# Down projection of an encoder block as one group of 22 pairs, with gate/up units of two k pairs

## The chip, the cores and the metric

The kernel runs on one core of one Trainium2 chip. The metric is the device time of one launch in microseconds. The core has a matrix engine (TensorE, PE in the profile; its weight loads are PEld), VectorE (DVE), ScalarE (ACT), GpSimd (POOL), and SyncE (SP), which here only issues transfers. Each engine works through its own instructions in order; semaphores order the engines against one another.

## What is computed

One layer of an encoder on x of 512 tokens by 2048 channels, in float32: a normalised input projection, two attention mixers, an output projection added to x, and a gated feed-forward block, then a last normalisation. The change touches the feed-forward block and the last normalisation:

```python
h2 = rmsnorm(x, g_ffn[layer])
gate, up = jnp.split(jnp.einsum('bsd,df->bsf', h2, w_gate_up[layer]), 2, axis=-1)
x = x + jnp.einsum('bsf,fd->bsd', jax.nn.silu(gate) * up, w_down[layer])
...
return rmsnorm(x, g_final)
```

The feed-forward width is 5632, that is 44 tiles of 128 ("f-tiles").

## The kernel before

**Precision.** Every float32 operand is split in two: `hi`, a copy in the matmul's float32r type made by ScalarE, and `lo`, the rest, made by VectorE. `mm3` (lines 194 to 196) issues three matmuls, hi·hi, hi·lo and lo·hi. One matmul has a stationary tile of 128 x 128 (tokens of one tile) and 512 moving weight columns.

**Seven products instead of eight.** Gate/up and most of down use Winograd's form of Strassen's scheme on 2 x 2 blocks: the tokens in two halves (tiles 0, 1 and 2, 3), the contraction in pairs of k tiles, the columns in two blocks of 512. `CHAIN` is the order of the seven products, m1, m7, m6, m2, m5, m4, m3. For each of them the activations have a "form" (a sum or difference of blocks, made by `pair_sums`), split in hi and lo and held in `arena`, two tiles of four pairs each; and each weight pair gives a column of its own: m1, m2 and m3 take a weight block as it is, m7, m6, m5 and m4 a difference or sum made by VectorE in place (`weights`, line 751). Results of several products are added up in the same PSUM banks without starting anew: m1, m6, m5, m3 in bank pair z, m7 and m4 in y, m2 in x. Between them the running value is read out, as every partial chain is one of the wanted terms.

**Units.** A list `units` is worked through in order. One `Cols` unit is one product of one pair: a 256 KB load (`Raw`, tag "craw", 24 buffers), its hi split on ScalarE (line 720) and lo split on VectorE (line 723) into one of eight `twin` buffers, and six matmuls (two token tiles by three). `prepare(n)` issues, ahead of unit n's matmuls, the loads of units up to 20 us ahead and the splits of those up to 8 us ahead, by an assumed 1.37 us per unit. `hooks` attach other work to a unit: evictions, sums, silu, transposes.

**Gate/up** (`gate_up_block`): 11 blocks of four f-tiles, each 7 products by 8 pairs = 56 units. In the units after a block its activations are multiplied, transposed on TensorE (`turn`), summed into the forms (`pair_sums`) and stored in DRAM (`forms_dram`) for the first 40 f-tiles; the last four f-tiles are stored plain (`act_dram`).

**Down.** The first 40 f-tiles are 20 pairs in groups of 8, 8 and 4 (`DOWN_PAIRS`), each group by two column blocks of 1024: six blocks of 7 products. `next_forms` loads the forms (512 KB chunks of four pairs, two buffers `fraw`) and splits them into `arena` (lines 877 and 880) while the block before still runs. The residual x1 lies in DRAM (`x1_dram`). After each product ScalarE reads out its two banks, scaled by the row's factor, into an `ev` slot (line 896), and POOL's queue adds it to x1 in DRAM with an accumulating store (line 897): 82 in all. At the end SP's queue reads x1 back (`load_x1`, line 865), and then the last four f-tiles are done as plain products (`last_down`, `finish`): 4 column chunks by 4 token tiles by 4 f-tiles by 3 = 192 matmuls, the last piece in halves, with the final normalisation beside them: x1 plus the product (line 953), its square sum (954), a product with g_final (961), the factor by a power on POOL, the scaling, and the stores.

Of the kernel before, what the change touches and what calls it, by code (L numbers as in the profile page):

```python
# [44 lines left out]
COLS_AHEAD = 8.0  # L45
COLS_LOAD = 20.0
COLS_US = 1.37
PLAIN_WAIT = 5
SPILL_B = 6
TWINS = 8  # L50
RAWS = {"raw": 6, "craw": 24}
W_TILES = {"wi": 12, "wo": 12, "wl": 32}
DOWN_PAIRS = (8, 8, 4)
F_PLAIN = 40
ORDER = ("m1", "m2", "m4", "m5", "m6", "m7", "m3")
# [7 lines left out]
def encoder_block(ctx, tc, x, g_mix, w_in, g_q_a, g_k_a, g_out_a, g_out_b, w_out, g_ffn,  # L63
# [48 lines left out]
    arena = [sp.tile([P, 7, 4, 2, 256], F32R, tag="arena", bufs=2, name=f"arena{i}") for i in range(2)]  # L112

    def home(n):
        i = n // 7
        return arena[i // 4][:, n % 7, i % 4].rearrange("p a b -> p (a b)")
# [534 lines left out]
    def pair_sums(w):  # L651
        def part(n):
            return w[:, n * 256:(n + 1) * 256]
        a_r, a_l, b_l, b_r, s1, s2, s3, s4 = (part(n) for n in range(8))

        def tt(out, x, y, op=OP.subtract):
            nc.vector.tensor_tensor(out, x, y, op=op)
        tt(s1, a_r, b_r, OP.add)
        tt(s3, a_l, a_r)
        tt(s2, s1, a_l)  # L660
        tt(s4, b_l, s2)

    def form_of(form, i):
        m = ORDER.index(form)
        return arena[i // 4][:, m, i % 4, 0], arena[i // 4][:, m, i % 4, 1]
# [4 lines left out]
    def h_side(i, half, apart=False):  # L670
        if half < 2:
            k = 2 * i + half
            c, j = divmod(k, 4)
            ps = bank("x1t")
            for n, t in enumerate((2, 3, 0, 1) if half == 0 else range(NT)):
                nc.tensor.transpose(ps[:, n * P:(n + 1) * P], x1[c][t][:, j * P:(j + 1) * P], ident)
            if half == 0:
                hpart[0] = sp.tile([P, 4 * 512], F32, tag="pair", bufs=1, name=nm("pair"))
            nc.scalar.activation(hpart[0][:, half * 512:(half + 1) * 512], ps, AF.Copy, scale=gf[:, k:k + 1])
        if half == 1:  # L680
            pair_sums(hpart[0])
        if half >= 2:
            src = hpart[0][:, 256:].rearrange("p (f c) -> p f c", c=256)
            hi, lo = (arena[i // 4][:, :, i % 4, j] for j in range(2))
            if half == 2:
                nc.scalar.activation(hi, src, AF.Copy)
            if half == 3 or not apart:
                nc.vector.tensor_tensor(lo, src, f32(hi), op=OP.subtract)  # L688
# [16 lines left out]
    act_dram = [dp.tile([P, 512], F32, tag=f"act{f}", name=f"act{f}") for f in range(F_PLAIN, NFF)]  # L705
    forms_dram = dp.tile([P, 7, F_PLAIN // 2, 256], F32, tag="forms", name="forms")

    class Cols(Unit):
        ahead = COLS_AHEAD
        load_ahead = COLS_LOAD  # L710
        dur = COLS_US

# [4 lines left out]
        def split_hi(self):  # L717
            self.src = self.box.weights(self.form, self.i)
            self.pair = sp.tile([P, 2, 512], F32R, tag="twin", bufs=TWINS, name=nm("tw"))
            nc.scalar.activation(self.pair[:, 0], self.src, AF.Copy)  # L720

        def split_lo(self):
            nc.vector.tensor_tensor(self.pair[:, 1], self.src, f32(self.pair[:, 0]), op=OP.subtract)  # L723
# [4 lines left out]
    class ColBlock:  # L728
        def __init__(self, w, row, lo, pairs, ready=None):
            self.pairs, self.ready = pairs, ready  # L730
            self.ps, self.at = {}, {}

            def raw(i, j, q):
                at = row + (2 * q + i) * P
                return Raw(lambda t: [(w[0, at:at + P, lo[j]:lo[j] + 512], t)], tag="craw", width=512)
            kinds = {"a": (0, 0), "b": (0, 1), "c": (1, 1), "d": (1, 0), "e": (0, 1), "f": (1, 0), "g": (1, 1)}
            self.raws = [{n: raw(i, j, q) for n, (i, j) in kinds.items()} for q in range(pairs)]
            need = {"m1": "a", "m7": "cb", "m6": "ba", "m2": "d", "m5": "ea", "m4": "fb", "m3": "g"}
            order = [(form, q) for form in CHAIN for q in range(pairs)]
            if ready is not None:  # L740
                rest = order[6:8] + order[8:3 * pairs] + order[3 * pairs + 6:]
                order = order[:6] + order[3 * pairs:3 * pairs + 6] + rest
            for form, q in order:
                self.at[form] = len(units)
                units.append(Cols(self, form, q, [self.raws[q][n] for n in need[form]]))

        def weights(self, form, q):
            t = {n: r.t for n, r in self.raws[q].items()}
# [7 lines left out]

        def bank_of(self, form):
# [5 lines left out]
        def multiply(self, u):  # L763
            dst, i = self.bank_of(u.form), u.i
            if self.ready is not None:
                drain_until(lambda: self.ready[i])
            for t in range(2):
                mm3(dst[t], cols(form_of(u.form, i), t * P), (u.pair[:, 0], u.pair[:, 1]),
                    u.form in ("m1", "m7", "m2") and i == 0, i == self.pairs - 1, True)
# [4 lines left out]
    def gate_up_block(f0):  # L774
        box = ColBlock(w_gate_up, 0, (f0 * P, DFF + f0 * P), KD // 2, hf if f0 == 0 else None)
# [34 lines left out]
        def turn(k):  # L810
            ps = bank("at")
            half = k % 2
            for n, t in enumerate((2, 3, 0, 1) if half == 0 and f0 + k < F_PLAIN else range(NT)):
                src = st[("glo", "uhi")[t // 2]][:, t % 2, k * P:(k + 1) * P]
                nc.tensor.transpose(ps[:, n * P:(n + 1) * P], src, ident)
            if f0 + k >= F_PLAIN:
                a = slot("actT")
                nc.scalar.activation(a, ps, AF.Copy)
                nc.sync.dma_start(act_dram[f0 + k - F_PLAIN], a)
                return  # L820
            if half == 0:
                st["pair"] = sp.tile([P, 4 * 512], F32, tag="pair", bufs=1, name=nm("pair"))
            nc.scalar.activation(st["pair"][:, half * 512:(half + 1) * 512], ps, AF.Copy)

        def store(n):
            nc.sync.dma_start(forms_dram[:, :, n], st["pair"][:, 256:].rearrange("p (f c) -> p f c", c=256))
# [5 lines left out]
        silu("m2", 4, "glo", 0)  # L832
        add("m5", 1, "s7", "uhi")
        add("m4", 1, "s6", "ghi")
        silu("m4", 4, "ghi", 1)
        box.after("m3", 1, low)
        box.after("m3", 3, high)
        for k in range(4):
            late = (6, 8, 18, 20)[k]
            box.after("m3", late, lambda k=k: turn(k))  # L840
            if k % 2 and f0 + k < F_PLAIN:
                box.after("m3", late + 2, lambda: pair_sums(st["pair"]))
                box.after("m3", late + 7, lambda k=k: store((f0 + k) // 2))
        return box

    for f in range(0, NFF, 4):
        box = gate_up_block(f)

    act = {}

    class Act:
        def __init__(self, f):
            self.f, self.t = f, None

        def load(self):
            self.t = slot("actf")
            nc.sync.dma_start(self.t, act_dram[self.f - F_PLAIN])

        def split(self):
            act[self.f] = split(self.t, "act")  # L860

    def load_x1(c, rows):
        for t in rows:
            x1.setdefault((c, t), slot("x1"))
            nc.sync.dma_start(x1[c, t], x1_dram[c, t])

    def next_forms(box, first, pairs):
        def ready(form, h):
            m, st = ORDER.index(form), {}
            hi, lo = (arena[h][:, m, :, j] for j in range(2))  # L870

            def load():
                st["t"] = sp.tile([P, 4, 256], F32, tag="fraw", bufs=2, name=nm("fr"))
                nc.sync.dma_start(st["t"], forms_dram[:, m, first + 4 * h:first + 4 * h + 4])

            def split_hi():
                nc.scalar.activation(hi, st["t"], AF.Copy)

            def split_lo():
                nc.vector.tensor_tensor(lo, st["t"], f32(hi), op=OP.subtract)  # L880
            box.after(form, 3 * h - 5, load)
            box.after(form, 3 * h + 1, split_hi)
            box.after(form, 3 * h + 3, split_lo)
        for form in CHAIN:
            for h in range(pairs // 4):
                ready(form, h)

    def down_block(first, pairs, cb, last):
        box = ColBlock(w_down, 2 * first * P, (cb * 1024, cb * 1024 + 512), pairs)

        def add(form, late, i, j):
            def go():
                for t in range(2):
                    row = 2 * i + t
                    e = slot("ev")
                    nc.scalar.activation(e, box.bank_of(form)[t], AF.Copy, scale=r2["r"][:, row:row + 1])  # L896
                    nc.gpsimd.dma_start(x1_dram[2 * cb + j, row], e, accum_op=OP.add)  # L897
            box.after(form, late, go)

        def close():  # L900
            for t in range(2):
                dst = x1[2 * cb + 1, t]
                nc.vector.scalar_tensor_tensor(dst, box.bank_of("m3")[t], r2["r"][:, t:t + 1], dst,
                                               op0=OP.mult, op1=OP.add)
        add("m1", 0, 0, 0)
        add("m7", 0, 1, 1)
        add("m6", 0, 1, 0)
        add("m2", 0, 0, 0)
        add("m5", 0, 1, 1)
        add("m4", 0, 1, 0)  # L910
        if last:
            box.after("m4", -1, lambda: load_x1(3, (0, 1)))
# [208 lines left out]
```

## Time and profile before

| what | before |
|---|---|
| runs | 2056.56, 2057.41, 2057.89 us; median 2057.41 |
| span of the profiled execution (the only time that the profile gives for it) | 2057.2 us |
| matmuls and transposes on TensorE | 9159 |
| last matmul starts | 2048.61 us |
| moved by DMA | 386.39 MB, mean 188 GB/s |

How to read it: a matmul's shown duration overlaps with that of the next, so the pace is read from the starts. The profile's times count from the first instruction. In a row of groups the columns are line, engine, operation, tiles and shapes with the count, then busy us and the mean ns of one, then the idle time of that engine ahead of the group with what ended it. In a row of waits they are the waiting instruction, what released it, and total, number and longest of these waits in us. PEclk is the clock granted to TensorE, 1.00 being full.

### The profile page before, as it was taken

What the parts mean: (1) busy time and instruction counts of PE and PEld (TensorE: products, weight loads), DVE (VectorE), ACT (ScalarE), POOL (GpSimd) and SP (SyncE); (2) the same over time, 40 slices, a digit from 0 to 9 for tenths busy, and PEclk for the clock granted to TensorE, in tenths of its full rate; (3) what the DMA queues carried; (4) which work ended last, traced back from release to release, by engine and by line L of the source; (5) the groups of instructions that cost most, each with busy time, mean ns of one, the idle gap of its engine ahead of it and who ended that gap; (6) DMA issues with size and microseconds to landing.
All of it is one profiled execution on the core that took longest, in us unless ns stands there. A gap on an engine that the chain in (4) does not pass through costs nothing.

```text
span 2057.2 us, 27020 instructions
## 1 busy us (share of the span) xinstructions
PE 2022.3 (98%) x9159; PEld 1660.1 (81%) x9159; DVE 1462.2 (71%) x2566; ACT 1047.1 (51%) x1854; POOL 129.1 (6%) x135
## 2 busy tenths in 40 slices
PE   9999999999999999999999999999999999999897
PEld 7888888888888878888888888888887888788675
DVE  5555755645654698877877878878879878877565
ACT  5334344444534565554555554554556666566453
POOL 3100100000000000000000000000000111111220
PEclk9999999999999999999999999999999999999999
DMA  7322222222433654845835836836748989989974
GB/s 231 109 76 83 87 74 76 73 82 92 153 119 134 214 164 162 309 135 192 316 122 207 299 124 222 288 121 236 274 138 311 276 247 331 315 236 314 241 178 151
DMA packets 227978, 386.39 MB, mean 188 GB/s; under 512 B 20944, under 2 KB 64000, under 8 KB 227840
## 3 DMA queue, kind: packets, MB, share of 16 engines
q1 hardware_dynamic: 213840, 359.43, 51.3%
q0 software_dynamic: 11808, 21.50, 6.5%
q10 hardware_dynamic: 2192, 3.74, 0.5%
q8 instruction: 71, 1.16, 0.2%
q14 instruction: 67, 0.55, 0.1%
HBM read 331.64 MB, written 52.95 MB: 187 GB/s over the span
## 4 chain that ended last, share of the span: by engine, by line
PE 85%; issue 7%; DMA 4%; DVE 2%; POOL 2%; ACT 1%; SPq 0%; POOLq 0%; ACTq 0%; DVEq 0%
PE zc L196 9%; PE zc L194 9%; PE zc L195 9%; PE pj L194 6%; PE pj L195 6%; PE pj L196 6%; PE yc L195 5%; PE yc L196 5%; PE yc L194 5%; PE pw L194 3%; PE pw L196 3%; PE pw L195 3%; PE xc L196 2%; PE xc L195 2%; PE xc L194 2%
## 5 line engine op out<-in xcount | busy, mean ns | idle before, releaser
L720 ACT ACTIVATE tw<-raw 128x512 fp32r<-128x512 f32 x896 | 541.2, 629 | 410.0 <-DVE raw L751 285.2
L723 DVE TENSOR_TENSOR tw<-raw,tw 128x512 fp32r<-128x512 f32 x896 | 599.4, 687 | 206.2 <-ACT tw L720 198.5
L194 PE MATMUL zc<-tw,arena 128*128 128x512 f32 x1024 | 404.5, 395 | 6.2 <-ACT ev L896 6.1
L195 PE MATMUL zc<-tw,arena 128*128 128x512 f32 x1024 | 400.8, 391 | 0.2
L196 PE MATMUL zc<-tw,arena 128*128 128x512 f32 x1024 | 400.9, 392 | 0.0
L751 DVE TENSOR_TENSOR raw<-raw,raw 128x512 f32<-128x512 f32 x512 | 350.8, 685 | 0.0
L194 PEld LDWEIGHTS zc<-tw,arena 128*128 128x128 f32 x1024 | 193.4, 189 | 47.8 <-ACT ev L896 8.6
L194 PE MATMUL pj<-w,arena 128*128 128x512 f32 x576 | 229.3, 398 | 1.2 <-ACT w L232 1.2
L195 PEld LDWEIGHTS zc<-tw,arena 128*128 128x128 f32 x1024 | 193.5, 189 | 41.4 <-DVE tw L723 2.3
L196 PEld LDWEIGHTS zc<-tw,arena 128*128 128x128 f32 x1024 | 193.2, 189 | 41.1 <-DVE arena L688 0.4
L195 PE MATMUL pj<-w,arena 128*128 128x512 f32 x576 | 225.4, 391 | 0.9 <-DVE w L237 0.9
L196 PE MATMUL pj<-w,arena 128*128 128x512 f32 x576 | 225.7, 392 | 0.0
L194 PE MATMUL yc<-tw,arena 128*128 128x512 f32 x512 | 201.2, 393 | 4.4 <-ACT tw L720 4.4
L195 PE MATMUL yc<-tw,arena 128*128 128x512 f32 x512 | 200.9, 392 | 2.4 <-DVE tw L723 2.4
L196 PE MATMUL yc<-tw,arena 128*128 128x512 f32 x512 | 200.0, 391 | 0.0
L237 DVE TENSOR_TENSOR w<-raw,w 128x512 fp32r<-128x512 f32 x192 | 140.8, 747 | 27.0 <-ACT w L232 19.2
L232 ACT ACTIVATE w<-raw 128x512 fp32r<-128x512 f32 x192 | 116.1, 627 | 67.5 <-PE pj L196 29.4
L897 POOL DMA_DIRECT2D x1d<-ev x82 | 72.4, 951 | 1177.8 <-ACT ev L896 1169.4
L194 PEld LDWEIGHTS pj<-w,arena 128*128 128x128 f32 x576 | 108.6, 189 | 23.8 <-ACT w L232 1.4
L196 PEld LDWEIGHTS pj<-w,arena 128*128 128x128 f32 x576 | 108.5, 188 | 23.8 <-DVE arena L189 0.2
L195 PEld LDWEIGHTS pj<-w,arena 128*128 128x128 f32 x576 | 108.7, 189 | 23.4 <-DVE w L237 1.2
L194 PEld LDWEIGHTS yc<-tw,arena 128*128 128x128 f32 x512 | 96.5, 189 | 25.5 <-ACT tw L720 5.7
(189 smaller groups left out, 2633.7 us busy)
## 6 DMA issues: line engine op xcount, KB each, us to landing
raw<-in_w_gate_up_dram SPq DMA_DIRECT2D x616, 256.0 KB, 5.4
raw<-in_w_down_dram SPq DMA_DIRECT2D x280, 256.0 KB, 6.9
x1d<-ev POOLq DMA_DIRECT2D x82, 256.0 KB, 6.8
raw<-in_w_in_dram SPq DMA_DIRECT2D x38, 512.0 KB, 3.8
forms<-pair SPq DMA_DIRECT2D x20, 896.0 KB, 5.3
fr<-forms SPq DMA_DIRECT2D x35, 512.0 KB, 6.0
raw<-in_w_in_dram SPq DMA_DIRECT2D x68, 256.0 KB, 3.0
raw<-in_w_out_dram SPq DMA_DIRECT2D x32, 512.0 KB, 4.2
```

The source lines that it names most:

```text
L194: nc.tensor.matmul(dst, ah, bh, start=start, stop=False, skip_group_check=chained)
L195: nc.tensor.matmul(dst, ah, bl, start=False, stop=False, skip_group_check=chained)
L196: nc.tensor.matmul(dst, al, bh, start=False, stop=stop, skip_group_check=chained)
L232: nc.scalar.activation(self.w[0], src, AF.Copy)
L237: nc.vector.tensor_tensor(self.w[1], self.src, f32(self.w[0]), op=OP.subtract)
L720: nc.scalar.activation(self.pair[:, 0], self.src, AF.Copy)
L723: nc.vector.tensor_tensor(self.pair[:, 1], self.src, f32(self.pair[:, 0]), op=OP.subtract)
L751: nc.vector.tensor_tensor(t[d], t[a], t[b], op=op)
L897: nc.gpsimd.dma_start(x1_dram[2 * cb + j, row], e, accum_op=OP.add)
```

## The change

What it does:

- **Down**: all 44 f-tiles are 22 pairs in one group (`Down`). A unit covers one product of one pair for both column blocks: weights `[P, 2, 512]`, loaded as 512 KB, and 12 matmuls. Products run in braids of two, m1 with m7, m6 with m4, m5 with m2, the second eight pairs behind the first, then m3 alone. The eight banks are z (m1, m6, m5, m3) and y (m7, m4, then m2).
- The block a of each weight pair stays in SBUF from m1 to m5 (`home`, 22 tiles); m7 turns it in place into the column that m6 takes (`between`). All other down loads share the 12 places of three `stock` tiles.
- Forms are loaded in chunks of four pairs just ahead of their use into four `forms_at` tiles.
- m1, m7, m6 and m4 are read out with four accumulating stores each, 16 in all, through two `evs` tiles. m5 and m2 are added from PSUM to x1 tiles, which POOL's queue loads, with g_final, near the end of m5.
- The last four pairs of m3 are held back and done by token tile in `finish`, the last piece in halves in banks of y.
- **Gate/up**: units of two k pairs (`Wides`): 512 KB loads into stock tiles a, b and s of four places each, splits of 128 x 1024, 12 matmuls, four twins. Hooks count in the new units; the arena is divided by form (four and three forms) instead of by pair.

```diff
-DOWN_PAIRS = (8, 8, 4)
-F_PLAIN = 40
-ORDER = ("m1", "m2", "m4", "m5", "m6", "m7", "m3")
+COLS_AHEAD = 8.2
+WIDE_US = 2.72
+PAIRS = NFF // 2
+LAG = 8
+TAIL = 4
+CHUNK = 4
+ORDER = ("m1", "m4", "m5", "m3", "m2", "m7", "m6")
...
+    stock = {k: wp.tile([P, 4, 2, 512], F32, tag="stock" + k, bufs=1, name="stock" + k) for k in "abs"}
+    twins = [sp.tile([P, 2, 2, 512], F32R, tag=f"twin{k}", bufs=1, name=f"twin{k}") for k in range(4)]
...
+        def load(self):
+            if self.tag == "home":
+                self.t = wp.tile([P, 2, 512], F32, tag="home", bufs=PAIRS, name=nm("home"))
+            else:
+                n = turns[self.tag]
+                turns[self.tag] += 1
+                self.t = stock["abs"[n // 4 % 3] if self.tag == "d" else self.tag][:, n % 4]
+            nc.sync.dma_start(self.t, self.src)
...
         def split_hi(self):
             self.src = self.box.weights(self.form, self.i)
-            self.pair = sp.tile([P, 2, 512], F32R, tag="twin", bufs=TWINS, name=nm("tw"))
-            nc.scalar.activation(self.pair[:, 0], self.src, AF.Copy)
+            n = turns["twin"]
+            turns["twin"] += 1
+            self.pair = twins[n % 4]
+            nc.scalar.activation(self.pair[:, :, 0], self.src, AF.Copy)
 
         def split_lo(self):
-            nc.vector.tensor_tensor(self.pair[:, 1], self.src, f32(self.pair[:, 0]), op=OP.subtract)
+            self.box.between(self.form, self.i)
+            nc.vector.tensor_tensor(self.pair[:, :, 1], self.src, f32(self.pair[:, :, 0]), op=OP.subtract)
...
+            for lead, lag in (("m1", "m7"), ("m6", "m4"), ("m5", "m2")):
+                for q in range(PAIRS + LAG):
+                    if q < PAIRS:
+                        order.append((lead, q))
+                    if q >= LAG:
+                        order.append((lag, q - LAG))
+            order += [("m3", q) for q in range(PAIRS)]
...
+            return {"m1": lambda: a, "m7": lambda: tt(t["b"], t["c"], t["b"]), "m6": lambda: a,
+                    "m4": lambda: tt(t["d"], t["d"], a), "m5": lambda: tt(t["c"], t["c"], a),
+                    "m2": lambda: t["d"], "m3": lambda: t["c"]}[form]()
+
+        def between(self, form, q):
+            if form == "m7":
+                a = self.home[q].t
+                nc.vector.tensor_tensor(a, self.raws[form, q]["b"].t, a, op=OP.add)
...
+            hook(first - 7, load)
+            hook(first - 3, hi)
+            hook(first - 2, lo)
...
+            for cb in range(2):
+                e = evs[turns["ev"] % 2][:, cb]
+                nc.scalar.activation(e, box.bank_of(form)[t][cb], AF.Copy, scale=r2["r"][:, row:row + 1])
+                nc.gpsimd.dma_start(x1_dram[2 * cb + j, row], e, accum_op=OP.add)
...
+    for n in range(4):
+        box.after("m5", PAIRS - 4, n, lambda n=n: take_x1(4 * n, 4 * n + 4))
+    box.after("m5", PAIRS - 2, 1, load_gfin)
...
+        add_in(z[1][1], 3, 1)
+        for cb in range(2):
+            run(z[0][cb], 0, cb, 0, 512, False)
+            add_in(z[0][cb], 2 * cb + 1, 0)
+            square(2 * cb + 1, 0)
+        rows_done(0)
+        run(z[1][0], 1, 0, 0, 512, False)
+        for c in (1, 3):
+            give(c, 0)
+        scale_out(0, rf[0])
+        add_in(z[1][0], 1, 1)
+        square(1, 1)
...
+        for n, (lo, hi) in enumerate(((0, 256), (256, 512))):
+            run(y[0][n], 1, 1, lo, hi, True)
+            add_in(y[0][n][:, lo:hi], 3, 1, lo, hi)
...
+            if n == 0:
+                nc.vector.tensor_tensor(early_y1, xd[1, 1], gf_of(1), op=OP.mult)
+                nc.vector.tensor_reduce(pre[:, :1], ssf[:, 4:8], axis=AX.X, op=OP.add)
+                nc.vector.tensor_scalar(pre[:, 1:], pre[:, :1], 1.0 / D, EPS, op0=OP.mult, op1=OP.add)
```

418 lines of the change are left out of this document (229 added, 189 removed).

## The prediction, made before the changed kernel was run

> **What bounds the kernel now.** I read the page first: engine totals, then the largest groups.
>
> ```profile
> span 2057.2 us, 27020 instructions
> PE 2022.3 (98%) x9159; PEld 1660.1 (81%) x9159; DVE 1462.2 (71%) x2566; ACT 1047.1 (51%) x1854; POOL 129.1 (6%) x135
> ```
>
> TensorE (PE) has hardly an idle moment, so only two things can shorten the span: fewer matmuls, or matmuls that start closer together. How close they can be is in the timeline of TensorE in an undisturbed gate/up block (start, duration):
>
> ```profile
> 1005.67 0.39 PE L194 MATMUL zc<-tw,arena 128*128 128x512 f32 x1
> ...
> 1016.55 0.39 PE L194 MATMUL yc<-tw,arena 128*128 128x512 f32 x1
> ```
>
> Between these starts lies one product of a block: eight units of six matmuls, 48 in 10.88 us, **0.2267 us each**. The 0.39 us is the overlapped duration, which is why a busy share of 98% can hide losses. So I cut the stretch from the last gate/up block's m2 to the last matmul into windows (window, length, PE busy (count), PEld, DVE, ACT, POOL, PEclk, DMA share, GB/s) and set each length against its matmuls at 0.2267 us:
>
> ```profile
> 1541.44:1588.81 47.37, 45.52 (x193) 35.57 (x192) 46.27 (x71) 31.97 (x51) 0.00 (x0) 1.00 0.86 301
> 1588.81:1753.96 165.15, 165.15 (x738) 136.71 (x736) 132.42 (x202) 99.42 (x162) 24.96 (x28) 1.00 0.96 287
> 1753.96:1767.24 13.28, 11.75 (x49) 8.85 (x48) 11.11 (x18) 7.62 (x13) 1.76 (x2) 1.00 1.02 342
> 1767.24:1908.68 141.44, 141.44 (x625) 117.16 (x624) 108.96 (x171) 83.53 (x137) 23.84 (x27) 1.00 0.98 282
> 1908.68:1923.70 15.02, 12.20 (x50) 8.59 (x48) 7.50 (x12) 7.14 (x12) 2.62 (x4) 1.00 1.08 329
> 1923.70:1956.86 33.16, 27.59 (x97) 20.84 (x97) 19.81 (x32) 17.58 (x30) 8.71 (x10) 0.85 0.89 188
> 1956.86:1979.08 22.22, 22.19 (x98) 17.87 (x96) 12.23 (x20) 10.38 (x18) 5.26 (x6) 1.00 1.00 273
> 1979.08:1996.12 17.04, 13.06 (x49) 10.07 (x48) 8.18 (x14) 11.07 (x21) 3.48 (x4) 0.90 0.59 81
> 1996.12:2048.61 52.49, 46.21 (x205) 37.61 (x203) 35.33 (x62) 22.16 (x52) 3.42 (x5) 0.93 0.48 150
> 2048.61:2057.20 8.59, 0.28 (x3) 0.07 (x1) 2.13 (x6) 1.84 (x4) 0.55 (x1) 0.81 0.35 122
> ```
>
> Losses, row by row: 192 matmuls need 43.5, 3.8 lost; the second row none (720 matmuls, 163.2, and 16 transposes); 48 need 10.9, 2.4 lost; 624 need 141.5, none; 48: 4.1; 96 (21.8): 11.4; 96: 0.4; 48: 6.1; the last row has 180 whole matmuls and 24 half ones, 43.5, about 8.9 lost. Together **37.1 us**, all in the last gate/up block and the down stage, and in part a lower granted clock (PEclk 0.85 to 0.93) where TensorE had paused. The waits name the causes. First the window of the last two down blocks and the end (waiter <- releaser: total, times, longest), then the window of the last gate/up block:
>
> ```profile
> DVE tw L723 <- ACT tw L720: 44.0, 14, 5.1
> ACT ev L896 <- DMA x1d<-ev: 27.3, 17, 4.1
> PE fd L194 <- ACT w L232: 6.1, 1, 6.1
> PE zc L194 <- ACT ev L896: 6.1, 3, 3.8
> ```
>
> ```profile
> L880 DVE TENSOR_TENSOR arena<-fr,arena 128x1024 fp32r<-128x1024 f32 x9 | 11.0, 1218 | 0.0
> PE yc L195 <- DVE tw L723: 1.3, 3, 0.7
> ```
>
> In the short last blocks (four pairs, 38 us) ScalarE stands 27.3 us before evictions whose buffer an accumulating store still holds; the weight splits queue behind them, VectorE waits for the splits and TensorE for both. Then the read-back of x1 delays the weights of the last four f-tiles (6.1). In the last gate/up block nine splits of down forms add 11.0 us to a VectorE that is busy 46.27 of 47.37.
>
> **The change, part by part.** *Last four f-tiles as two more pairs.* 192 matmuls of the plain product and 1680 of 20 pairs become 22 x 7 x 12 = 1848: 24 fewer, 24 x 0.2267 = **-5.4**. The extra instructions from a halved last piece are 12 before and after: 0.
>
> *Gate/up units of two k pairs.* Same matmuls and bytes, so 0 from this part on TensorE, which has no gaps there. VectorE gains cover. Its timeline shows what an operation really occupies:
>
> ```profile
> 1550.86 0.68 DVE L751 TENSOR_TENSOR raw<-raw,raw 128x512 f32<-128x512 f32 x1
> 1551.46 0.68 DVE L723 TENSOR_TENSOR tw<-raw,tw 128x512 fp32r<-128x512 f32 x1
> 1552.06 1.22 DVE L880 TENSOR_TENSOR arena<-fr,arena 128x1024 fp32r<-128x1024 f32 x1
> 1553.20 0.68 DVE L751 TENSOR_TENSOR raw<-raw,raw 128x512 f32<-128x512 f32 x1
> ```
>
> Start to start a narrow operation takes 0.60 and a wide one **1.14**, less than their durations. A wide unit with a difference costs 2.28 of the 2.72 us that its 12 matmuls take (84%; two narrow ones 2.40). Four twins and three units ahead are as much time as before. The loads c to g of a block share four slots ("s"). The tightest is e: it waits until d of the same index is split, and its difference must start four units later; from 2.4 us into one unit (when that second split ends, below) to 1.2 us before the start of the fourth unit after it are 4 x 2.72 - 3.6 = 7.3 us.
>
> ```profile
> raw<-in_w_gate_up_dram SPq DMA_DIRECT2D x616, 256.0 KB, 5.4
> raw<-in_w_in_dram SPq DMA_DIRECT2D x38, 512.0 KB, 3.8
> raw<-in_w_out_dram SPq DMA_DIRECT2D x32, 512.0 KB, 4.2
> ```
>
> Loads of 512 KB land in 3.8 to 4.2 us, so it holds, with VectorE's lead as a second cover. If that cover were gone it would cost the lateness once per block.
>
> *Form splits leave the last gate/up block* but for one: **-3.8**, and VectorE there falls below TensorE's need.
>
> *Accumulating stores 82 to 16, two buffers of their own.* After each of m1, m7, m6, m4 four evictions, two per unit, at least eight units (21.8 us) before the bank or the buffer is needed again. Stores land in 6.8 us (first row below). The waits for ev, and the pauses behind them, go; so does the read-back in front of weights: x1 and g_final, 5.2 MB, move from SP's queue, where weights stood behind them, to POOL's, where only the accumulating stores, long done, are ahead; 17 issues of 0.95 us run from four units before m5's last one, while weights and forms there ask 241 GB/s (one load of 512 KB and a quarter of a chunk per unit) of the 390 shown below. **-33.3**, the rest of the 37.1.
>
> ```profile
> x1d<-ev POOLq DMA_DIRECT2D x82, 256.0 KB, 6.8
> L897 POOL DMA_DIRECT2D x1d<-ev x82 | 72.4, 951 | 1177.8 <-ACT ev L896 1169.4 <-DMA raw<-in_w_down_dram 7.2 <-DMA fr<-forms 1.2
> ```
>
> *What is late next: VectorE in the first braid.* m1 costs a split (1.14); m7 a difference, the in-place sum for m6, and a split (3.42); a form chunk 1.14 each four units. A pair of units is 4.56 + 0.57 = 5.13 of 5.44 us: it fits. But the braid ends with eight m7 units alone: 8 x 3.42 = 27.4, with chunk splits (1.14, 1.14, 0.6) 30.2, against 21.8 of TensorE: 8.4 short. A twin is free only when its matmuls are done, so a unit's second split ends about a unit start + 2.4 us, three units early: at most 8.16 - 2.4 = 5.8 us of lead. Shortfall 2.6; the last chunk falls into slack behind, and I take **+2.0**. Bounds: 0, if chunks fall outside; 8.4 with no lead.
>
> A rule of the Trainium skill would make this dearer. The page "VectorE: DVE Perf Modes", section "The DRAIN you can't avoid", says the next operation does not start until the pipe has emptied. By it each step takes its full duration, 1.22 us; this gives the rival of full steps below. The rows above show a start 0.08 us before the former's end, so I keep 1.14.
>
> *DMA in that braid.* Three loads of 512 KB per two units and half a chunk are 1.84 MB in 5.44 us, 337 GB/s; the last eight units ask 434 for 21.8 us, with twelve slots filled ahead. What the engines give with the same 2 KB pieces, in one window:
>
> ```profile
> 1000.00:1010.88 10.88, 10.88 (x49) 9.01 (x48) 10.35 (x18) 4.99 (x9) 0.00 (x0) 1.00 1.06 390
> ```
>
> 390 suffices with the slots. The Trainium skill's "DMA: Bandwidth & Descriptors", section "Where 436 GB/s comes from", has HBM bind at about 358 per core; by that figure the braid still fits and the tail lacks 1.6 MB, less than the slots hold. The window is above it.
>
> *The end.* Four m3 units are held back for the finish. At pair 18 the last unit's first split must wait for pair 17's matmuls: 1.05 (first row below) + 1.14 and hand-overs, about 2.6 us, while only nine matmuls (2.0) are left: +0.5. In the finish the scaling of rows t=0 (two operations each on ScalarE and VectorE) stands before t=1's sums, and the partial mean before the last addition: by the durations below the latter is ready some 0.9 us after the last matmul. **+1.4** together, between 0 and 3. The chain after that is the same operations as now: 0.
>
> ```profile
> L877 ACT ACTIVATE arena<-fr 128x1024 fp32r<-128x1024 f32 x35 | 36.9, 1053 | 8.0 <-DMA fr<-forms 8.0
> L953 DVE SCALAR_TENSOR_TENSOR x<-fd,r,x 128x512 f32<-128x512 f32 x15 | 11.2, 748 | 5.8 <-PE fd L196 5.8
> L961 DVE TENSOR_TENSOR y<-x,gfin 128x512 f32<-128x512 f32 x15 | 10.4, 693 | 3.4 <-DMA gfin<-in_g_final_dram 2.1 <-ACT jf L954 0.8
> ```
>
> *Handing memory over.* Stock tiles are bigger single tiles, home tiles lie where the arena's halves were, and a pair's split becomes two pieces per engine. The wait at the change to gate/up is now
>
> ```profile
> PE x1t L676 <- DVE x L621: 0.7, 2, 0.4
> ```
>
> and I add as much again, **+0.7**, from 0 to 4: a load that waits for memory is issued seven units ahead, and the split of a pair in two pieces is hidden behind the out projection for all but the last pair.
>
> Sum: 2057.2 - 5.4 - 3.8 - 33.3 + 2.0 + 1.4 + 0.7 = 2018.8. The median of the runs, 2057.41, is 0.2 above this execution: **2019.0**.
>
> **The rivals.** *Full steps* (5%): at 1.22 us a pair of units takes 5.49 of VectorE against 5.44, which costs 0.7 of lead over 14 pairs, and the eight units with their chunk splits 32.4 against 21.8: 10.6 short, less 5.1 of lead, +5.5 in place of +2.0, **2022.5**. Against: the spacing shown.
>
> *VectorE or the read-back decides* (17%): no lead remains at the m7 tail (+6.4), or x1 and g_final, 5.2 MB beside the weights, cost again the 6.1 that they cost now: 2025. For: VectorE at 5.13 of 5.44 us has no reserve; against: four units between a load's issue and its use.
>
> *DMA bounds the first braid* (13%). Windows of down with accumulation beside it move 282 to 342 GB/s. At 300 each pair of units takes 6.1 instead of 5.44, 9.5 over 14 pairs, and the eight alone 31.5 instead of 21.8, 9.7; the slots' 6.3 MB give some back: up to +19, say +14, with a lowered clock near 2034. Against: 390 without accumulation, of which the first braid has none until its end.
>
> *Slower than before* (4%): the four shared slots. If a 512 KB load landed later than about 7.3 us plus VectorE's 4.6 of free lead, each of the 11 gate/up blocks would stop at its m5. To lose all 38.4 that is 3.5 us per block: it decides from a landing of 11.9 us and turns the sign at 15.4. No median among the rows above is over 6.8. A further 2% is the stalls returning in full elsewhere: within 0.2%.
>
> **How the numbers follow.** Forecast 59% (2014 to 2023), full steps 5%, 2025: 17%, 2034: 13%, same 2%, slower 4%. The range takes forecast and the first rival, and the near part of the second: from 2013.5 (all losses gone and no new one is 2015.1; 1.6 less if wide units shorten the start of gate/up) to 2031. Faster by over 0.2%, about 4 us and what this kernel's runs can tell from none, 94%.
>
> **What would show it.** Right: 0.2267 us between matmuls from 30 us to the end but for some 2 us at the last m7 units, where TensorE waits for VectorE's second split; 24 fewer matmuls; PEclk 1.00 until the last matmul; no waits for ev buffers. Wrong: ScalarE or VectorE waiting for a weight load in the first braid (DMA), pauses in each gate/up block's m5 (slots), or a pause at the x1 loads.

## The result and the profile after

| | before | changed |
|---|---|---|
| four runs of each, median (lowest to highest) | 2057.30 us (2056.56 to 2057.89) | 2023.15 us (2022.11 to 2024.27) |
| span of the profiled execution | 2057.2 us | 2022.5 us |
| last matmul starts | 2048.61 us | 2013.31 us |

The ratio of the times is 0.9834 (95% interval 0.9820 to 0.9848): 1.7% faster. The forecast was 2019.0 us in a range of 2013.5 to 2031. The page of the changed kernel begins:

```profile
span 2022.5 us, 24151 instructions
...
PE 2005.3 (99%) x9135; PEld 1653.4 (82%) x9135; DVE 1429.0 (71%) x1876; ACT 952.6 (47%) x1345; POOL 81.7 (4%) x86
```

TensorE has 9135 instructions for 9159: the 24 matmuls are gone. The windows of the changed kernel, with the columns of the windows before (window, length, PE, PEld, DVE, ACT, POOL, PEclk, DMA share, GB/s), cover the start of gate/up, one whole gate/up block, its last block's m2 to m3, and down to the end:

```profile
742.89:762.36 19.47, 15.90 (x60) 12.30 (x58) 16.29 (x19) 10.16 (x15) 1.86 (x1) 0.82 0.38 140
...
1468.23:1546.35 78.12, 78.12 (x354) 64.63 (x352) 60.20 (x62) 37.26 (x43) 0.00 (x0) 1.00 0.64 212
1546.35:1589.87 43.52, 43.52 (x194) 36.04 (x192) 33.13 (x32) 20.88 (x23) 0.00 (x0) 1.00 0.94 328
1589.87:1686.94 97.07, 97.07 (x437) 80.49 (x436) 90.08 (x86) 48.18 (x50) 0.49 (x1) 1.00 0.92 329
1686.94:1713.63 26.69, 25.64 (x109) 20.03 (x108) 26.69 (x25) 14.16 (x17) 3.78 (x5) 1.00 0.74 218
1713.63:1952.99 239.36, 239.36 (x1057) 198.20 (x1056) 185.50 (x163) 125.39 (x139) 19.14 (x29) 1.00 0.76 253
1952.99:2010.56 57.57, 57.42 (x254) 47.22 (x253) 41.23 (x49) 28.38 (x36) 2.66 (x3) 1.00 0.45 151
2010.56:2013.31 2.75, 2.75 (x25) 2.75 (x23) 2.67 (x5) 1.90 (x4) 0.05 (x1) 1.00 0.39 145
2013.31:2022.50 9.19, 0.28 (x3) 0.07 (x1) 2.46 (x7) 2.41 (x8) 0.54 (x1) 0.64 0.54 185
```

Read each length against its matmuls at 0.2267 us. The last gate/up block's 192 matmuls take 43.52 us, just what they need; they took 47.37 before. In 239.36 us of down there are 1056, which need 239.4: nothing lost, and the clock stays at 1.00. Only four places are not at pace: nine m7 units at the end of the first braid (108 matmuls, 24.5 needed, 26.7 taken: 2.2), the last product (0.4), the end behind the last matmul (9.19 for 8.59), and, not in down at all, the start of gate/up, where 19.47 us hold 60 records and the granted clock is 0.82 in the mean. TensorE's own waits name two of them:

```profile
PE zc L196 <- ACT arena L700: 3.5, 1, 3.5
...
PE yd L197 <- DVE twin L754: 0.9, 3, 0.4
```

So the 37.1 us of old losses are gone, and a new pause of 3.8 us between starts has come at 743 us: TensorE waits there for ScalarE's split of a form.

### The profile page after: what moved, and what is told of

Read it like the earlier page. It is cut to its first block, busy times and chain, and to the rows that moved or that the text cites. A ratio compares the mean times of both kernels' runs of the same rounds, so it can differ in the third digit from the quotient of the medians.

```text
span 2022.5 us, 24151 instructions
## 1 busy us (share of the span) xinstructions
PE 2005.3 (99%) x9135; PEld 1653.4 (82%) x9135; DVE 1429.0 (71%) x1876; ACT 952.6 (47%) x1345; POOL 81.7 (4%) x86
## 4 chain that ended last, share of the span: by engine, by line
PE 95%; DVE 3%; issue 1%; ACT 1%; DMA 0%; ACTq 0%; POOLq 0%; POOL 0%; DVEq 0%
PE zc L198 8%; PE zc L196 8%; PE zc L197 8%; PE pj L196 7%; PE pj L198 7%; PE pj L197 7%; PE yc L196 4%; PE yc L198 4%; PE yc L197 4%; PE zd L197 4%; PE zd L198 4%; PE zd L196 4%; PE pw L196 3%; PE pw L198 3%; PE pw L197 3%; PE yd L198 3%
## 5 line engine op out<-in xcount | busy, mean ns | idle before, releaser
L196 PE MATMUL zc<-twin,arena 128*128 128x512 f32 x704 | 277.8, 395 | 3.5 <-ACT arena L700 3.5
L198 PE MATMUL zc<-twin,arena 128*128 128x512 f32 x704 | 275.3, 391 | 0.0
L197 PE MATMUL zc<-twin,arena 128*128 128x512 f32 x704 | 274.6, 390 | 0.0
L750 ACT ACTIVATE twin<-stockb 128x1024 fp32r<-128x1024 f32 x168 | 178.3, 1062 | 191.1 <-PE zc L198 76.9
L754 DVE TENSOR_TENSOR twin<-stockb,twin 128x1024 fp32r<-128x1024 f32 x168 | 205.1, 1221 | 40.8 <-ACT twin L750 38.8
L754 DVE TENSOR_TENSOR twin<-stocks,twin 128x1024 fp32r<-128x1024 f32 x126 | 154.2, 1224 | 103.6 <-ACT twin L750 103.2
L750 ACT ACTIVATE twin<-stocka 128x1024 fp32r<-128x1024 f32 x124 | 131.5, 1061 | 170.9 <-PE xc L198 58.3
L754 DVE TENSOR_TENSOR twin<-stocka,twin 128x1024 fp32r<-128x1024 f32 x124 | 151.5, 1223 | 66.5 <-ACT twin L750 58.5
L750 ACT ACTIVATE twin<-stocks 128x1024 fp32r<-128x1024 f32 x126 | 133.4, 1059 | 133.1 <-PE yc L198 71.4
L196 PEld LDWEIGHTS zc<-twin,arena 128*128 128x128 f32 x704 | 132.4, 188 | 30.7 <-ACT arena L700 3.8
L198 PEld LDWEIGHTS zc<-twin,arena 128*128 128x128 f32 x704 | 132.4, 188 | 28.9 <-DVE arena L702 0.8
L197 PEld LDWEIGHTS zc<-twin,arena 128*128 128x128 f32 x704 | 132.6, 188 | 26.3
L196 PE MATMUL yc<-twin,arena 128*128 128x512 f32 x352 | 138.6, 394 | 0.0
L198 PE MATMUL yc<-twin,arena 128*128 128x512 f32 x352 | 137.6, 391 | 0.0
L197 PE MATMUL yc<-twin,arena 128*128 128x512 f32 x352 | 137.5, 391 | 0.0
L197 PE MATMUL zd<-twin,form 128*128 128x512 f32 x348 | 135.5, 389 | 0.1
L196 PE MATMUL zd<-twin,form 128*128 128x512 f32 x348 | 135.6, 390 | 0.0
L198 PE MATMUL zd<-twin,form 128*128 128x512 f32 x348 | 135.4, 389 | 0.0
```

Of the source, the lines that this page charges most:

```text
L196: nc.tensor.matmul(dst, ah, bh, start=start, stop=False, skip_group_check=chained)
L197: nc.tensor.matmul(dst, ah, bl, start=False, stop=False, skip_group_check=chained)
L198: nc.tensor.matmul(dst, al, bh, start=False, stop=stop, skip_group_check=chained)
L750: nc.scalar.activation(self.pair[:, :, 0], self.src, AF.Copy)
L754: nc.vector.tensor_tensor(self.pair[:, :, 1], self.src, f32(self.pair[:, :, 0]), op=OP.subtract)
```

## The experiments

Unless it says otherwise a time is the span of one profiled execution, to be set against 2022.5 (changed) or 2057.2 us (before). Spans of one kernel differ by some us: the four of the changed kernel lie between 2020.3 and 2022.5, ten more of the kernel before between 2052.3 and 2056.4, so both figures are at the long end of their kind. In the runs below the part ahead of gate/up, which no edit touches, alone ends anywhere from 722.7 to 724.7 us. So where a span says one thing and the window of the edited stage another, the window decides.

### Where the new pause comes from

The last three times that TensorE makes a half-pair of the feed-forward input (four transposes in a row), from its timeline of the kernel before, then of the changed one:

```profile
728.88 0.60 PE L676 MATMUL x1t<-ident,x 128*128 128x128 f32 x4
734.80 0.60 PE L676 MATMUL x1t<-ident,x 128*128 128x128 f32 x4
736.62 0.60 PE L676 MATMUL x1t<-ident,x 128*128 128x128 f32 x4
```

```profile
729.69 0.60 PE L688 MATMUL x1t<-ident,x 128*128 128x128 f32 x4
741.06 0.60 PE L688 MATMUL x1t<-ident,x 128*128 128x128 f32 x4
742.89 0.60 PE L688 MATMUL x1t<-ident,x 128*128 128x128 f32 x4
```

These transposes are tasks of the `side` queue, which gives out one task after each unit. A unit has twice the matmuls now, so the queue runs at half its pace: from the first of the rows to the second, with other tasks between them, pass 5.9 us before and 11.4 after.

```diff
-        if side:
-            side.popleft()()
+        for _ in range(2 if isinstance(u, Wides) else 1):
+            if side:
+                side.popleft()()
```

> The changed kernel, with two tasks of the side queue per wide unit instead of one. Theory: the 3.8 us pause at 743 us and the slow restart come from the side queue, which gives out one task per unit while a unit is now twice as long, so that the last pair of the feed-forward input is transposed at 742.9 us instead of 736.6. Then the last transposes move to about 737 us, the pause goes, and the span falls from 2022.5 to about 2017.5 us. Rival: the pause comes from the new division of the arena or the split in two pieces; then the pause of 3 us or more stays and the span stays within 1 us of 2022.5.

Measured 2016.9 us, 5.6 less. The last transposes start at 736.39 us in its timeline. From the first matmul of gate/up to the end of the first m7 it takes 32.9 us, 5.7 less than the changed kernel. One wait of 1.05 us is left there, 12 matmuls (2.72 us) in 3.77:

```profile
742.30:746.07 3.77, 3.23 (x14) 2.10 (x12) 3.73 (x7) 3.09 (x5) 0.00 (x0) 1.00 1.05 404
```

The theory holds; the new division of the arena and the split in two pieces, which stay in this run, are not the cause of the 3.8 us.

### The end of the first braid

VectorE is busy for the whole of the window 1686.94 to 1713.63 above, 26.69 of 26.69 us. Its timeline there shows the spacing of the wide operations:

```profile
1697.56 1.21 DVE L917 TENSOR_TENSOR stocka<-stocka 128x1024 f32<-128x1024 f32 x1
1698.69 1.22 DVE L926 TENSOR_TENSOR home<-stocka,home 128x1024 f32<-128x1024 f32 x1
1699.83 1.21 DVE L754 TENSOR_TENSOR twin<-stocka,twin 128x1024 fp32r<-128x1024 f32 x1
1700.96 1.21 DVE L917 TENSOR_TENSOR stockb<-stockb 128x1024 f32<-128x1024 f32 x1
```

Difference, sum for m6, split, and the next unit's difference: starts 1.13 to 1.14 us apart, 3.40 us a unit where TensorE needs 2.72. Two runs test that VectorE, and not the loads, sets the pace. The first shortens the stretch in which m7 stands alone:

```diff
-LAG = 8
+LAG = 4
```

> The changed kernel with the second product of a braid four pairs behind the first instead of eight. Theory (VectorE is short in the m7 units that stand alone): with four alone the shortfall is 4 x 0.7 plus chunk splits, under the lead of 5.8 us, so the waits of TensorE for VectorE there (2.2 us) go: span about 2020.3. Rival (the first braid's weights come late): four units alone still ask for 434 GB/s, but for 10.9 us only; the waits would fall too, but ScalarE or VectorE would be seen waiting for a load.

Measured 2018.5 us. The window of its five m7 units at the end:

```profile
1695.66:1709.26 13.60, 13.60 (x62) 11.26 (x61) 13.56 (x13) 9.20 (x12) 3.79 (x5) 1.00 0.91 195
```

60 matmuls in 13.60 us is full pace, with VectorE busy 13.56 of them: the lead just suffices. The 2.2 us are gone: down takes 421.3 us from its first matmul to its last, where the changed kernel takes 423.4. The rest of the difference is not the edit's: 2.2 us less ahead of down, 0.4 more behind the last matmul. The second run adds to VectorE's work and to nothing else:

```diff
-                nc.vector.tensor_tensor(self.pair[:, :, 1], ...)
+            for _ in range(2 if self.form == "m7" and isinstance(self.box, Down) else 1):
+                nc.vector.tensor_tensor(self.pair[:, :, 1], ...)
```

> The changed kernel with the low split of each m7 unit of down done twice (same result). Theory (VectorE bounds the first braid, 1.14 us a step): a pair of braided units takes 6.27 of VectorE against 5.44, 11.6 over 14 pairs, and the eight alone with chunk splits 39.4 against 21.8; less 5.8 of lead that is 23.4 of waiting in place of 2.2, span about 2044. With steps of 1.22 us it would be near 2052. Rival (the weights' loads bound it): VectorE has room, span within 5 us of 2022.5.

Measured 2047.5 us, 25.0 more. The nine units, 24.5 us of matmuls, now take 42.4, with VectorE full and the DMA engines at half load:

```profile
1696.26:1738.64 42.38, 29.42 (x110) 20.73 (x108) 42.07 (x38) 16.27 (x19) 4.61 (x5) 0.96 0.54 155
```

That is VectorE's bound: 22 more operations at 1.14 us are 25.1 us, and 25.0 came (25.6 in down itself). My sum said 21. It let the lead cover all but 5.8 us of what the braid ahead of these nine units loses; there 107.0 us passed where the changed kernel takes 97.1, a loss of 10.0.

A third run took the sum off VectorE:

```diff
-                nc.vector.tensor_tensor(a, self.raws[form, q]["b"].t, a, op=OP.add)
+                nc.gpsimd.tensor_tensor(a, self.raws[form, q]["b"].t, a, op=OP.add)
```

> The changed kernel with the in-place sum that m7 leaves for m6 on GpSimd instead of VectorE. Theory: VectorE has then two steps per m7 unit, 2.28 of 2.72 us, and the 2.2 us at the end of the first braid go: span about 2020.3. If GpSimd's wide sum (a narrow one takes 1.29 us, so 2.6 or more) slows VectorE or comes late for m6: slower than 2022.5.

Measured 2048.2 us: a miss, 25.7 more instead of 2.2 less. VectorE's and GpSimd's timelines of that run:

```profile
1719.32 1.21 DVE L754 TENSOR_TENSOR twin<-stocka,twin 128x1024 fp32r<-128x1024 f32 x1
1720.45 3.39 DVE L917 TENSOR_TENSOR stockb<-stockb 128x1024 f32<-128x1024 f32 x1
1723.77 1.21 DVE L754 TENSOR_TENSOR twin<-stocka,twin 128x1024 fp32r<-128x1024 f32 x1
```

```profile
1719.53 3.23 POOL L926 TENSOR_TENSOR home<-stocka,home 128x1024 f32<-128x1024 f32 x1 [2.36 <-issue]
1723.93 3.32 POOL L926 TENSOR_TENSOR home<-stockb,home 128x1024 f32<-128x1024 f32 x1 [1.17 <-DVE stockb L917]
```

GpSimd's sum runs from 1719.53 to 1722.76. VectorE's difference starts in that time and takes 3.39 us in place of 1.21: it ends 1.1 us after the sum, as if it had begun only then. The relief was paid back with the time of the other engine's instruction. In the same run a split of 8.13 us stands beside three sums in a row; it ends 1.1 us after the last of them, which takes 2.44 us, the least of all 22 sums:

```profile
1710.13 8.13 DVE L754 TENSOR_TENSOR twin<-stocks,twin 128x1024 fp32r<-128x1024 f32 x1
1714.73 2.44 POOL L926 TENSOR_TENSOR home<-stocka,home 128x1024 f32<-128x1024 f32 x1
```

### What the old losses in down were

First four runs of the kernel before with one edit each, then one with two of these edits together and one of the changed kernel.

```diff
-                    e = slot("ev")
+                    e = sp.tile([P, 512], F32, tag="ev", bufs=8, name=nm("ev"))
```

> The kernel before, with eight buffers of their own for evictions instead of places among the shared slots. Theory (evictions wait for a buffer that an accumulating store holds, and the splits queue behind them): the 27.3 us of ScalarE's waits for buffers fall to a few, and of the 24 us lost in the last two down blocks most comes back: span 2057.2 to about 2037. Rival (the DMA engines are overloaded by accumulation and form loads, buffers are only where it shows): the wait moves to weight loads, span above 2050.

Measured 2033.0 us: 24.2 less from eight buffers of 2 KB per partition. The evictions' waits for a buffer held by a store are gone, and the blocks of four pairs, which had lost 22 us, run at pace, with all 82 accumulating stores still there and the DMA engines as busy as before: 312 of their 336 matmuls in 70.72 us (first row).

```profile
1906.24:1976.96 70.72, 70.72 (x314) 58.56 (x312) 53.40 (x87) 50.38 (x87) 22.63 (x26) 1.00 1.04 276
1731.52:1758.32 26.80, 23.55 (x98) 19.02 (x96) 14.85 (x23) 13.67 (x22) 3.54 (x4) 0.94 1.00 317
1976.96:2024.53 47.57, 45.56 (x205) 37.47 (x203) 32.18 (x56) 19.31 (x46) 1.66 (x3) 0.96 0.55 189
```

What is left, besides the last gate/up block, is a loss of 5.0 us from 1743 us on, between the second and the third block, where the first product waits for its banks to be read out (second row, 96 matmuls), and 4.0 us at the last four f-tiles (third row, 43.5 needed), of which TensorE's wait for the last weights is 2.0.

```diff
-                    nc.gpsimd.dma_start(x1_dram[2 * cb + j, row], e, accum_op=OP.add)
+                    nc.gpsimd.dma_start(x1_dram[2 * cb + j, row], e)
```

> The kernel before, with plain stores in place of the accumulating ones: leaves out the adding of down's products to x1. Theory of buffers held by accumulating stores: a plain store lands earlier, so the waits shrink but not wholly: span about 2040 to 2048. Rival (the number of stores and their issue on GpSimd's queue, not the accumulation): no less than 2052.

Measured 2039.0 us, 18.2 less, 1 us under the range expected. A plain store lands in 5.8 us, the accumulating one in 6.8, and ScalarE still waits 25.6 us for buffers in all of down (33.0 before). How long a buffer is held matters, but holding it less long helps less than giving the evictions buffers of their own. Whether more places among the shared slots would do as much was not run.

```diff
-            nc.sync.dma_start(x1[c, t], x1_dram[c, t])
+            nc.gpsimd.dma_start(x1[c, t], x1_dram[c, t])
```

> The kernel before, with x1 read back through GpSimd's queue instead of SyncE's, so that weight loads no longer stand behind it. Theory: the 6.1 us of TensorE's wait for the last weights go and no other: span about 2051. Rival (it is the DMA engines' time, not the queue): the wait stays, 2055 or more.

Measured 2048.7 us, 8.5 less. The whole of the loss at the last four f-tiles is gone, 8.9 us: they take 43.55 us where they took 52.49. (Gate/up began 1.2 us earlier, and 1.7 more were lost between.)

```profile
1996.54:2040.09 43.55, 43.55 (x205) 36.53 (x203) 34.52 (x61) 21.47 (x50) 11.07 (x19) 1.00 0.54 169
```

It was the order in SyncE's queue and not the DMA engines' time. I had counted the 6.1 us of waiting alone; the slow restart after it came on top: in the kernel before, right behind that wait, from 2012.38 to 2016.26 us, the matmuls start 0.32 to 0.73 us apart, at a granted clock of 0.50.

```diff
-DOWN_PAIRS = (8, 8, 4)
+DOWN_PAIRS = (4, 8, 8)
```

> The kernel before, with the group of four pairs first instead of last (4, 8, 8). Theory (pauses come from the short blocks, in which 14 stores fall into 38 us): the pauses move to the first two down blocks and the last ones run without; span within 8 us of 2057. Rival (they come from what happens at the end, the read-back of x1 among it): the pauses stay in the last 150 us.

Measured 2062.2 us. The pauses moved to where the short blocks went. Two windows: the first two blocks and the beginning of the third, then 576 of the 672 matmuls of the last two blocks:

```profile
1585.00:1720.00 135.00, 114.17 (x449) 85.15 (x449) 87.97 (x130) 74.48 (x118) 26.53 (x30) 0.95 0.93 259
1874.89:2005.44 130.55, 130.55 (x577) 108.11 (x576) 92.75 (x151) 73.06 (x123) 21.17 (x24) 1.00 0.93 255
```

In the second there is not one pause. So the 22 us belong to the short blocks, with their 14 evictions in 38 us, and not to the end of the kernel; here they are more, some 34 us up to the beginning of the third block. The last four f-tiles still lose 4.8 us (48.33 for 43.5).

The two edits together:

```diff
-                    e = slot("ev")
+                    e = sp.tile([P, 512], F32, tag="ev", bufs=8, name=nm("ev"))
...
-            nc.sync.dma_start(x1[c, t], x1_dram[c, t])
+            nc.gpsimd.dma_start(x1[c, t], x1_dram[c, t])
```

> The kernel before with eight buffers of their own for evictions and x1 read back through GpSimd's queue. Theory (the two waits are separate, and little of the second is left once the first is gone): 2033.0 less the 2.4 us that TensorE still waits at the last weights, about 2030.5. If the two gains add up in full, 24.2 and 8.5: 2024.5.

Measured 2030.5 us, the number expected, but in part by luck: the last four f-tiles got all of their 4.0 us back (43.55 for 47.57), not 2.4, and 0.7 us were lost ahead of gate/up and 0.8 between. The two gains do not add up, because the loss at the end is 8.9 us in the kernel before but only 4.0 with the eight buffers. That it shrinks because the stores ahead of it are through in time is an argument, not shown by a run.

And in the changed kernel, which has both fewer stores and buffers of their own, the buffers alone undone:

```diff
-                e = evs[turns["ev"] % 2][:, cb]
+                e = slot("ev")
```

> The changed kernel with its 16 evictions in places of the shared slots, as before the change, instead of two buffers of their own. Theory (with 16 stores at least eight units apart from the next use, buffers no longer matter): span within 1 us of 2022.5. Rival (the buffers of their own did it): 3 us slower or more.

Measured 2022.8 us, 0.3 more; down takes 423.5 us from first to last matmul, as in the changed kernel. ScalarE still waits twice for a buffer, but no longer at TensorE's cost:

```profile
ACT ev L998 <- DMA x1d<-ev: 7.0, 2, 4.6
```

### The last gate/up block before

```diff
             def split_lo():
-                nc.vector.tensor_tensor(lo, st["t"], f32(hi), op=OP.subtract)
+                pass
```

> The kernel before without the low splits of down's forms: leaves out the low part of down's activations. Theory (in the last gate/up block VectorE is full, and these 1.14 us splits are what is too much): the 3.8 us lost there go, and the 2.4 us at the second m7; span 2057.2 to about 2051. Rival (late loads of forms or weights): the 3.8 us stay, 2055 or more.

Measured 2048.2 us, 9.0 less, more than expected. The block's 192 matmuls from m2 to m3 are at full pace once VectorE is not full (34.63 of 43.52 us), although forms and weights load as before, at 343 GB/s:

```profile
1539.61:1583.13 43.52, 43.52 (x193) 36.04 (x192) 34.63 (x57) 31.55 (x49) 0.00 (x0) 1.00 0.99 343
```

That shows the 3.8 us to be VectorE's; the 2.4 us at the second group's m7 went too. Of the other 2.8 us 1.8 lie ahead of gate/up, which began at 722.65 us for 724.47; the last 1.0 was not followed up.

### The three small losses mended

Two side tasks per wide unit, a lag of four pairs, and in `finish` the partial mean moved behind the last addition:

```diff
-            if n == 0:
-                nc.vector.tensor_tensor(early_y1, xd[1, 1], gf_of(1), op=OP.mult)
-                nc.vector.tensor_reduce(pre[:, :1], ...)
-                nc.vector.tensor_scalar(pre[:, 1:], ...)
+            if n == 0:
+                nc.vector.tensor_tensor(early_y1, xd[1, 1], gf_of(1), op=OP.mult)
+        nc.vector.tensor_reduce(pre[:, :1], ...)
+        nc.vector.tensor_scalar(pre[:, 1:], ...)
```

> The changed kernel with three edits: two side tasks per wide unit, four pairs of lag in the braids, and the partial mean of the last row tile taken after the last addition instead of before it. Theory: the three losses found are separate, 5.3 us at the start of gate/up, 2.2 at the end of the first braid, 0.5 behind the last matmul; span 2022.5 less 8.0, about 2014.5. Rival (they cover one another): 2016 or more.

Measured over five runs 2015.96 us (2015.09 to 2017.15) against 2056.86 (2054.82 to 2058.67), ratio 0.9802 (0.9788 to 0.9816); span 2015.3 us, 7.2 under the changed kernel's. The windows of its five m7 units and of the end:

```profile
1692.96:1706.56 13.60, 13.60 (x61) 11.26 (x60) 13.57 (x13) 9.19 (x12) 3.78 (x5) 1.00 0.96 204
2006.28:2015.30 9.02, 0.28 (x3) 0.07 (x1) 2.38 (x7) 2.41 (x8) 0.55 (x1) 0.71 0.55 189
```

The first two losses are separate and go together: the start of gate/up takes 32.9 us for 38.6, down 421.2 for 423.4, and gate/up began 0.9 us later. The third edit works as expected, yet the end is at most 0.2 us shorter (9.02 for 9.19). The last addition now starts 0.32 us after the last matmul (2006.28) instead of 0.86 (2013.31), here first in this run and then in the changed kernel:

```profile
2006.60 0.48 DVE L1006 SCALAR_TENSOR_TENSOR xd<-yd,r,xd 128x256 f32<-128x256 f32 x1
2014.17 0.47 DVE L1006 SCALAR_TENSOR_TENSOR xd<-yd,r,xd 128x256 f32<-128x256 f32 x1
```

The gain is still there when the last stores are issued (2009.85 and 2017.36 us, 3.57 and 4.05 after the last matmul) and is lost behind that. Of this end the runs of the changed kernel whose edits leave it alone take 9.19 to 9.55 us. A wait of 1.05 us at the start of gate/up and 0.5 in the last product stay.

## Why the prediction was right, and where it was off

**The pace and the old losses (-37.1 us): right.** What the windows showed as lost did come back, and the experiments bear out each cause that the waits had named: buffers behind stores, the read-back ahead of weights, form splits on a full VectorE. Two things need saying beside that. The 2.4 us at the second group's m7 stand in the sum with the stores and the read-back (-33.3); the run without the low form splits shows that they go with the form splits. And the change as a whole was not needed for most of the gain: eight buffers in the kernel before bring 24.2 of the 34.7 us. Fewer stores and buffers of their own are two ways to the same end: the kernel before with eight buffers, and the changed kernel with its 16 evictions back in shared slots, show each alone to be enough to keep TensorE from waiting.

**24 matmuls (-5.4): right** by count and pace.

**Wide gate/up units (0): right in the steady state.** A whole block takes 78.12 us now; 336 matmuls at 0.2267 are 76.2, and the rest is 16 transposes. From the end of the first m7 to the first matmul of down it takes 827.5 us for 831.0, and the 3.5 less are the old loss of 3.8 in the last block.

**VectorE at the end of the first braid (+2.0): right**, 2.2 measured, in the place named, with VectorE full and the spacing of 1.14 us. The lead is as reckoned too: where both products run, a unit's second split ends at most 5.6 us ahead of its first matmul, for the 5.8 in the sum, and over the last nine units this lead falls from 4.1 us to nothing. The rival of full steps, +5.5, falls by the same rows; that the span is its 2022.5 is chance. The prediction took that rival from half a section: the Trainium skill's page "VectorE: DVE Perf Modes", section "The DRAIN you can't avoid", does say that the next operation does not start until the pipe is empty, but adds that a next operation which is not held starts earlier. The rows agree with this second sentence: 1.14 us from start to start, 1.21 to 1.22 in duration.

**DMA in the braid: right that it does not bind.** TensorE kept its pace with 329 GB/s moved (window 1589.87 to 1686.94), also from 1610 to 1670 us, where the DMA engines moved 384 to 392 GB/s at a share of 1.03 to 1.05. But I was wrong on the loads' landing, which I took as 3.8 to 4.2 us for 512 KB; the profile's page of the changed kernel has about twice that for some, and the one of the kernel before had 512 KB rows of 6.0 (forms) and 6.1 us (the last weights) already:

```profile
stocks<-in_w_gate_up_dram SPq DMA_DIRECT2D x220, 512.0 KB, 4.9
stocka<-in_w_gate_up_dram SPq DMA_DIRECT2D x44, 512.0 KB, 7.4
...
stocka<-in_w_down_dram SPq DMA_DIRECT2D x44, 512.0 KB, 9.0
```

The kinds that land late are issued further ahead, and cost nothing here. The tight kind, "s", lands in 4.9 us, under its 7.3, so the rival of four shared slots didn't come about.

**The end (+1.4): right in kind, 1.0 in size**, 0.4 at the held pairs (0.5 in the sum) and 0.6 behind the last matmul (0.9 in the sum); the last addition starts 0.86 us after the last matmul, and the run with three edits shows that the partial mean ahead of it is what delays it.

**Handing memory over (+0.7): the step that failed.** The start of gate/up cost 5.3 us: from its first matmul to the end of the first m7 it took 38.61 us (723.75 to 762.36) against 33.32 (724.47 to 757.79). That is outside the 0 to 4 that I gave for it. The size was wrong because the mechanism was: I looked for waits on memory, and wrote that the split in two pieces was hidden for all but the last pair. What made the last pair late was the emission loop, which hands out one side task per unit. The code for it was not in the diff, but its meaning changed when the unit grew to twice its length. The pause itself is 3.6 us more than a matmul's pace. After it the matmuls start 0.43 to 0.67 us apart until 752.71 us, at a granted clock of 0.50, 3.0 us more for twelve of them. Together that is more than the 5.3, since the kernel before is not at full pace in this stretch either. The window of the restart:

```profile
747.02:752.71 5.69, 5.65 (x12) 3.97 (x13) 5.66 (x8) 2.82 (x4) 1.86 (x1) 0.50 0.38 121
```

So the sign "PEclk 1.00 until the last matmul" failed at this place.

The sum: 2057.2 - 5.4 - 37.1 + 5.3 + 2.2 + 1.0 = 2023.2; the span is 2022.5, as gate/up began 0.7 us earlier. Nearly all of the distance from the forecast of 2019.0 is this one term. The range held, but it had been made wide for VectorE and the read-back, not for this. (Its lower end was worked from 2015.1, which should read 2014.9; nothing hangs on it.)

## What to carry to other kernels

Where an engine looks 98% busy, take the pace from the starts of its instructions in a clean stretch and set each window's length against its count; the difference is the most that a change of order can bring, and here nearly all of it came. Then ask of each wait for a buffer, before the loop is rebuilt, whether buffers of its own would do. When a unit of work grows, look at everything that counts in units: leads, hooks, and queues that advance once per unit.

## What the runs showed of the hardware that was not expected

A wide sum of two SBUF tensors mostly takes 3.1 to 3.3 us on GpSimd beside a busy VectorE, and a VectorE operation with two SBUF inputs that starts while it runs ends only some 1.1 us after it: 3.39 us in place of 1.21. The Trainium skill's page "SBUF — State Buffer", section "SBUF: two separate sides", states this: the two engines share a port pair as an exclusive lock, also for a VectorE operation with two SBUF inputs against a GpSimd one that reads SBUF. The rows of the run with the sum on GpSimd agree with it. My expectation for that run named a slower VectorE as the other outcome, but gave it no price.
